# Storing the low parts of the first MLP's and the first pointwise convolution's weights in DRAM at their first use, and loading them at the second

## The chip, the cores and the metric

One core of a Trainium2 chip runs the whole program. The metric is the device time in microseconds (us). The profile is of one execution of that core; its engines are PE (TensorE, matrix products), DVE (VectorE), ACT (ScalarE), POOL (GpSimd) and SP (SyncE, which here only issues DMA transfers).

## The reference, cut to what matters

A network of two layers over 1024 tokens with 1024 channels, in float32. Layer 0 is a hybrid mixer (RWKV-7 time mixing beside sliding-window attention) and an MLP; layer 1 is a Conformer convolution and an MLP; a last rmsnorm ends it. The change touches the weights of these two parts:

```python
def conformer_conv(h, pw1_w, pw1_b, dw_w, dw_b, ln_g, ln_b, pw2_w, pw2_b):
    u = h @ pw1_w + pw1_b                                     # 1024 -> 2048
    u = u[..., :D_MODEL] * jax.nn.sigmoid(u[..., D_MODEL:])
    u = <depthwise convolution of 31 taps over tokens>(u, dw_w) + dw_b
    u = jax.nn.silu(<layer norm>(u))
    return u @ pw2_w + pw2_b

def sqrelu_mlp(h, w1, w2):                                    # 1024 -> 4096 -> 1024
    return jnp.square(jax.nn.relu(h @ w1)) @ w2
```

## The kernel before

Activations lie feature-major: a tile holds 128 channels by 512 tokens, so the 1024 tokens are worked on as two halves. To keep float32 accuracy each operand of a product is split into a high part in the reduced format (`hi`, a cast on ACT, L286 for weights) and a low part (`lo = x - hi`, the subtraction at L271 on DVE or POOL), and each product is three: high by high, high by low, low by high (`mm3`, L299 to L301).

Weights are never kept. `weights` (L273) loads a block in two **pieces** of 128x512 (256 KB each, from SP's queue), casts each on ACT into `whi` and subtracts into `wlo` on DVE or POOL. `wraw`, `whi` and `wlo` are rings of four slots, one piece each. A piece feeds twelve products. Which engine subtracts is set by `dve`: True is DVE, False is POOL, None lets a counter `nlo` choose DVE two times in three.

Since each half of the tokens goes through the network on its own, each weight is loaded and split twice. The order of the program from about 500 us on is

- the MLP of layer 0 on the first half (`mlp(0, x0)`, subtractions by the counter), woven on PE with the recurrence scans and the attention of both halves, to about 1040 us;
- `conv_in` of the first half (the first pointwise product, 16 blocks, and the gate `u`, L1217);
- the MLP of layer 0 on the second half (`mlp(0, x1)`, subtractions all on POOL), from 1151.65 to about 1563 us. Beside it DVE runs `conv`, the 31 taps (L1223 and L1226) of eight channel blocks, 240 of them L1226, for the first half, and then the layer norm, whose first product on PE is L1239;
- `conv_out` of the first half, and `conv_in` of the second half from about 1607 us;
- the MLP of layer 1 on the first half (its other weights, on POOL as well) from about 1699 us, with the second half's taps beside it on DVE; then the rest, to 2519 us.

An MLP goes by blocks of 512 hidden channels. `first` makes four hidden tiles of 24 products each (called F below): ACT squares them, and the low part `hidl` is subtracted at L271 on POOL. `second` makes eight output tiles in pairs of 24 products (called S0S1 to S6S7); each is added by DVE into `x` at L1183, an addition with one operand in PSUM and one in SBUF, after which its PSUM slot is free. There are six slots. The order in PE's queue is F0 F1 of the next block, S0 to S7 of this one, F2 F3 of the next one; so S6 may start when DVE has added S0, F2 when it has added S2, and the next F0 when it has added S4.

The order of each queue is settled when the kernel is built (on PE by hand to 1040 us, else by the scheduler), and no engine changes it while it runs. On POOL stands also L1457, which copies the last 30 columns of a finished `u` to its front, as soon as the taps of that channel block are done.

Of the kernel before, what the change touches and what calls it, by code (L numbers as in the profile page):

```python
# [9 lines left out]
F32 = mybir.dt.float32  # L10
F32R = mybir.dt.float32r
# [6 lines left out]
P = 128  # L18
# [15 lines left out]
class Ring:  # L34
    """slots taken in turn, from one or several pools"""
# [10 lines left out]
class Net:  # L46
    def __init__(self, ctx, tc, A, out):
        self.ctx, self.tc, self.nc, self.A, self.out = ctx, tc, tc.nc, A, out
        self.nlo = 0
        self.clk = 0.0  # L50
        self.done = set()
        self.natt = 0
        self.open = []

# [17 lines left out]
    # ---------------------------------------------------------------- order on the tensor engine  # L72
    def go(self, gen):
        """a stream on its own"""
        while True:
            try:
                next(gen)
            except StopIteration as e:
                return e.value

    def weave(self, base, *gens):
        """several streams in one order: the first of gens that is due goes on, base between them, so that the array
        stays busy; a stream yields the time (us) that its next products have to wait for the other engines, or the
        name of what has to be there"""
# [22 lines left out]
    # ---------------------------------------------------------------- constants  # L107
# [62 lines left out]
    def warm(self):  # L170
        """products that nobody reads, while the array would only wait: so its clock stays up for the first columns"""
# [92 lines left out]
    # ---------------------------------------------------------------- helpers  # L264
    def lo(self, out, x, hi, dve=None):
        """out = x - hi, for the second part of an operand"""
# [6 lines left out]
    def weights(self, aps, a, b, dve=None):  # L273
        """blocks of weights in two parts, k by k; loaded and split one half of them after the other"""
        nc = self.nc
        h = a // 2
        if dve is None:
# [3 lines left out]
        for i in range(2):  # L281
            for ap, (his, los) in zip(aps, ws):
                raw = self.wraw.tile([P, h, b], F32, "wraw")
                nc.sync.dma_start(out=raw, in_=ap[:, i * h:(i + 1) * h, :])
                hi = self.whi.tile([P, h, b], F32R, "whi")
                nc.scalar.copy(out=hi, in_=raw)  # L286
                lo = self.wlo.tile([P, h, b], F32R, "wlo")
                self.lo(lo, raw, hi, dve)
# [4 lines left out]
    def weight(self, ap, a, b, dve=None):  # L293
        return self.weights([ap], a, b, dve)[0]
# [27 lines left out]
    def norm_first(self, hf, rows, dst):  # L322
        """first rmsnorm by rows, then turned to feature-major; dst(u, g): where the two parts go"""
# [42 lines left out]
    def first_stored(self):  # L366
        """the second half's first norm, kept in DRAM until its place is free"""
# [20 lines left out]
    def colsum(self, xs, sq, k="n"):  # L388
        """sum over channels of x (or of its square), in two parts"""
# [29 lines left out]
    def rstd(self, accs, eps, pool, k="n"):  # L419
        """1 / sqrt(mean + eps) for every token, on every partition"""  # L420
# [56 lines left out]
    # ---------------------------------------------------------------- input projection  # L477
# [10 lines left out]
    def w_in_pair(self, js, hs):  # L488
        """two columns side by side, channel block by channel block: what is there first is used first"""
# [31 lines left out]
    # ---------------------------------------------------------------- rwkv  # L521
    def scan(self, hf, p, r, k, v, la, gl, sset, ptag, ahead):
# [86 lines left out]
        # unit lower triangular inverse: 16-blocks by substitution, then two merges  # L609
# [97 lines left out]
        # per chunk: state' = M state + C, output = R state + Y  # L707
# [114 lines left out]
    # ---------------------------------------------------------------- attention  # L822
    def attention(self, hf, i, z, qs, mi):
        """query heads 2i and 2i+1"""
# [54 lines left out]
    # ---------------------------------------------------------------- mixer of one half  # L879
# [14 lines left out]
    def shift(self, hf, j, ps, keep=False, hp=False):  # L894
        """one 128-channel column of the input projection of the rwkv part, shifted"""
# [18 lines left out]
    def twice(self, j, rows, cols, width):  # L914
        """64 channels of a column, on both halves of the partitions; cols: (from, of which half's column) pieces"""
# [6 lines left out]
    def att_in(self, hf):  # L922
        """keys with one block of the half before in front: the high part of each kv head on both halves of the
        partitions, the low parts of the first on the upper one and of the second on the lower one; values by rows"""
# [23 lines left out]
    def queries(self, hf, i, z):  # L948
        """two heads' queries, each with its high part on the half of the partitions where the low part of its keys is
        and its low part on the other one"""  # L950
# [10 lines left out]
    def att(self, hf, z):  # L961
        """attention of one half: query heads 4z to 4z+3"""
# [26 lines left out]
    def cols0(self, hs):  # L989
        """the first half's input projection"""  # L990
# [23 lines left out]
    def last1(self, h1):  # L1014
        """the last two columns, under the norm"""
# [20 lines left out]
    def scans(self, z, todo):  # L1036
        """scans one after the other in one set of tiles"""
# [39 lines left out]
    def w_out(self, hf, mi, xs, w_):  # L1077
        """output projection; the second half's input is there, the first half's comes along;
        the first half's first two columns begin with what is done, while the last scan and the attention go on"""
# [56 lines left out]
    # ---------------------------------------------------------------- mlp  # L1136
    def mlp(self, layer, halves, blocks, ahead, dve=None, close=None):
        """halves: list of (x tiles, (hi, lo)); blocks of 512 hidden channels;
# [365 lines left out]
```

## Time and profile before

| | us |
|---|---|
| three timed runs | 2516.49, 2522.08, 2525.11 (median 2522.08) |
| profiled execution, span of the instructions | 2519.2 |
| PE busy | 2355.4 (93%) |
| DVE busy | 1568.6 (62%) |
| ACT busy | 1055.3 (42%) |
| POOL busy | 843.9 (33%) |
| DMA, mean rate | 94 GB/s, 236.19 MB |

The page gives no time of the profiled execution beside its span, which lies among the three runs, 2.9 us under their median. On the page the span is cut into 40 slices of 63 us; a digit is the busy share in tenths, PEclk the granted clock of TensorE. A busy PE is one whose products overlap; the count of products in a stretch tells more than its busy share, and a chain or a wait names the instruction that was waited for.

### The profile page before, as it was taken

The numbers are of one execution on the slowest core, as the hardware profiler recorded it, in microseconds if no ns is written. First come the engines' busy times: TensorE is split into PE (matmuls) and PEld (weight loads), VectorE is DVE, ScalarE is ACT, GpSimd is POOL, SyncE is SP. The second block draws the span as 40 slices with busy tenths as digits, with TensorE's granted clock in tenths as the row PEclk, the third lists the DMA queues.
The fourth block names the chain that finished last, engine by engine and source line by source line (L and its number), as shares of the span: only waits on it lengthen the run. The fifth ranks groups of instructions, "written<-read, shape, count | busy, mean of one in ns | idle before, by whom it ended". The sixth has DMA issues, their size and how long they took to land.

```text
span 2519.2 us, 38162 instructions
## 1 busy us (share of the span) xinstructions
PE 2355.4 (93%) x14525; PEld 1875.1 (74%) x14525; DVE 1568.6 (62%) x2613; ACT 1055.3 (42%) x1888; POOL 843.9 (33%) x676
## 2 busy tenths in 40 slices
PE   7999899899999999999678999997779999999998
PEld 6776677767777778777566888876657888888887
DVE  6766745647573646499998403899998025533333
ACT  6546645445352424344223543523225434433333
POOL 2223333111111112126547664226456643212221
PEclk9999999989999999999898999999889999999999
DMA  6435324313122223323112333332222332433332
GB/s 210 115 108 147 93 67 147 101 58 90 56 70 85 74 81 101 101 84 101 59 59 76 101 98 99 93 88 84 67 67 80 101 100 88 127 100 96 97 99 85
DMA packets 371851, 236.19 MB, mean 94 GB/s; under 512 B 39522, under 2 KB 355156, under 8 KB 371668
## 3 DMA queue, kind: packets, MB, share of 16 engines
q1 hardware_dynamic: 367604, 225.89, 30.2%
q0 software_dynamic: 2176, 4.19, 0.6%
q10 hardware_dynamic: 1888, 3.67, 0.4%
q8 instruction: 114, 1.87, 0.3%
q14 instruction: 69, 0.57, 0.1%
HBM read 215.35 MB, written 18.35 MB: 93 GB/s over the span
## 4 chain that ended last, share of the span: by engine, by line
PE 64%; DVE 28%; ACT 3%; DMA 3%; issue 2%; SPq 0%; POOL 0%; ACTq 0%; DVEq 0%; POOLq 0%
PE mm L299 19%; PE mm L300 18%; PE mm L301 18%; DVE acc L1226 17%; DVE x L1183 1%; DVE wlo L271 1%; DVE nt L472 1%; PE sc L603 1%; DMA raw<-p 1%; PE sc L685 1%; DVE E L662 1%; DVE C L660 1%; DVE h L271 1%; PE sc L768 1%; PE at L842 1%
## 5 line engine op out<-in xcount | busy, mean ns | idle before, releaser
L271 POOL TENSOR_TENSOR wlo<-wraw,whi 128x512 fp32r<-128x512 f32 x448 | 630.6, 1411 | 1293.6 <-ACT whi L286 1223.3
L286 ACT CAST whi<-wraw 128x512 fp32r<-128x512 f32 x720 | 445.1, 620 | 1065.8 <-PE mm L300 911.0
L299 PE MATMUL mm<-h,whi 128*128 128x512 f32 x1792 | 730.3, 408 | 10.7 <-DVE x L1183 7.1
L301 PE MATMUL mm<-h,wlo 128*128 128x512 f32 x1792 | 707.2, 395 | 7.5 <-DVE wlo L271 7.5
L300 PE MATMUL mm<-h,whi 128*128 128x512 f32 x1792 | 706.4, 394 | 0.5 <-DVE h L271 0.3
L299 PE MATMUL mm<-hidh,whi 128*128 128x512 f32 x992 | 396.0, 401 | 77.0 <-DVE x L1183 75.4
L1226 DVE SCALAR_TENSOR_TENSOR acc<-u,par,acc 128x512 f32<-128x512 f32 x480 | 466.7, 1030 | 0.1
L299 PEld LDWEIGHTS mm<-h,whi 128*128 128x128 f32 x1792 | 340.5, 190 | 93.6 <-issue 18.1
L301 PEld LDWEIGHTS mm<-h,wlo 128*128 128x128 f32 x1792 | 340.4, 190 | 85.3 <-DVE wlo L271 11.6
L301 PE MATMUL mm<-hidh,wlo 128*128 128x512 f32 x992 | 389.8, 395 | 11.2 <-POOL wlo L271 11.2
L300 PEld LDWEIGHTS mm<-h,whi 128*128 128x128 f32 x1792 | 341.3, 190 | 67.8 <-issue 2.0
L300 PE MATMUL mm<-hidl,whi 128*128 128x512 f32 x992 | 390.0, 394 | 0.3 <-DVE hidl L271 0.2
L1183 DVE TENSOR_TENSOR x<-mm,x 128x512 f32<-128x512 f32 x248 | 167.6, 685 | 291.9 <-PE mm L301 291.7
L271 DVE TENSOR_TENSOR wlo<-wraw,whi 128x512 fp32r<-128x512 f32 x272 | 194.6, 717 | 202.7 <-ACT whi L286 194.4
L299 PEld LDWEIGHTS mm<-hidh,whi 128*128 128x128 f32 x992 | 189.3, 191 | 123.1 <-issue 80.7
L301 PEld LDWEIGHTS mm<-hidh,wlo 128*128 128x128 f32 x992 | 189.1, 191 | 52.2 <-POOL wlo L271 11.6
L300 PEld LDWEIGHTS mm<-hidl,whi 128*128 128x128 f32 x992 | 189.6, 191 | 39.8 <-issue 1.1
L271 POOL TENSOR_TENSOR hidl<-rel,hidh 128x512 fp32r<-128x512 f32 x77 | 113.1, 1468 | 44.3 <-ACT hidh L1162 25.1
L1158 ACT ACTIVATE rel<-rel 128x512 f32<-128x512 f32 x128 | 80.6, 632 | 3.5
L1157 ACT ACTIVATE rel<-mm 128x512 f32<-128x512 f32 x128 | 75.5, 592 | 5.9 <-DVE u L1217 4.8
L1164 DVE CAST hidh<-rel 128x512 fp32r<-128x512 f32 x68 | 31.4, 464 | 52.5 <-ACT rel L1158 52.4
L473 ACT CAST h<-nt 128x512 fp32r<-128x512 f32 x48 | 29.7, 621 | 56.9 <-DVE nt L472 56.5
(357 smaller groups left out, 2257.3 us busy)
## 6 DMA issues: line engine op xcount, KB each, us to landing
wraw<-in_mlp_w_dram SPq DMA_DIRECT2D x512, 256.0 KB
wraw<-in_cv_pw_w_dram SPq DMA_DIRECT2D x96, 256.0 KB
wraw<-in_hy_w_in_dram SPq DMA_DIRECT2D x80, 256.0 KB
wraw<-in_hy_w_out_dram SPq DMA_DIRECT2D x32, 256.0 KB
p<-stg SPq DMA_DIRECT2D x30, 256.0 KB
raw<-p SPq DMA_DIRECT2D x40, 128.0 KB
krv<-p SPq DMA_DIRECT2D x18, 256.0 KB
xrow<-in_x_dram SPq DMA_DIRECT2D x8, 512.0 KB
```

Of the source, the lines that this page charges most:

```text
L271: eng.tensor_tensor(out=out, in0=x, in1=hi.bitcast(F32), op=ALU.subtract)
L286: nc.scalar.copy(out=hi, in_=raw)
L299: mm(ps, lhsT=whi, rhs=xhi, start=start, stop=False)
L300: mm(ps, lhsT=whi, rhs=xlo, start=False, stop=False)
L301: mm(ps, lhsT=wlo, rhs=xhi, start=False, stop=stop)
L472: nc.vector.scalar_tensor_tensor(out=t, in0=xs[c], scalar=self.pv(gname, c), in1=r, op0=ALU.mult, op1=ALU.mult)
L473: nc.scalar.copy(out=his[c], in_=t)
L1157: nc.scalar.activation(out=t, in_=ps, func=AF.Relu)
L1158: nc.scalar.activation(out=t, in_=t, func=AF.Square)
L1164: nc.vector.tensor_copy(out=hi, in_=t)
L1183: nc.vector.tensor_tensor(out=x, in0=pss[o], in1=x, op=ALU.add)
L1226: nc.vector.scalar_tensor_tensor(out=acc, in0=u[:, j:j + H], scalar=self.pv(f"dw{j}", c), in1=acc, op0=ALU.mult, op1=ALU.add)
```

## The change

`weights` gets a mode `keep`. With "put" it does what it did, and then SP also writes each low piece into a DRAM tile of its own (256 KB). With "get" it loads the piece and casts the high part as before, and takes the low part by a second DMA from that DRAM tile instead of the subtraction. `mlp(0, x0)` and the first half's `conv_in` put, `mlp(0, x1)` and the second half's `conv_in` get: 128 and 32 pieces. In "get" the counter `nlo` isn't advanced. Nothing else is computed in another way.

```diff
     def weights(self, aps, a, b, dve=None, keys=None, keep=None):
         nc = self.nc
         h = a // 2
-        if dve is None:
+        if dve is None and keep != "get":
             self.nlo += 1
             dve = self.nlo % 3 != 0
         ws = [([], []) for _ in aps]
         for i in range(2):
-            for ap, (his, los) in zip(aps, ws):
+            for n, (ap, (his, los)) in enumerate(zip(aps, ws)):
                 raw = self.wraw.tile([P, h, b], F32, "wraw")
                 nc.sync.dma_start(out=raw, in_=ap[:, i * h:(i + 1) * h, :])
+                lo = self.wlo.tile([P, h, b], F32R, "wlo")
+                if keep == "get":
+                    nc.sync.dma_start(out=lo.bitcast(F32), in_=self.los.pop((keys[n], i)))
                 hi = self.whi.tile([P, h, b], F32R, "whi")
                 nc.scalar.copy(out=hi, in_=raw)
-                lo = self.wlo.tile([P, h, b], F32R, "wlo")
-                self.lo(lo, raw, hi, dve)
+                if keep != "get":
+                    self.lo(lo, raw, hi, dve)
+                if keep == "put":
+                    d = self.dp.tile([P, h, b], F32, name="lo", tag=f"lo{len(self.los)}", bufs=1)
+                    self.los[keys[n], i] = d
+                    nc.sync.dma_start(out=d, in_=lo.bitcast(F32))
...
-            yield from self.mlp(0, [(self.x0, n0)], range(8), 0)
+            yield from self.mlp(0, [(self.x0, n0)], range(8), 0, keep="put")
...
-        self.go(self.mlp(0, [(x1, self.norm(x1, "nf0", 1))], range(8), 2, False))
+        self.go(self.mlp(0, [(x1, self.norm(x1, "nf0", 1))], range(8), 2, False, keep="get"))
...
+            keep = "get" if hf else "put"
-            whi, wlo = self.weight(w[:, :, (NK + c) * P:(NK + c + 1) * P], NK, P)
+            whi, wlo = self.weight(w[:, :, (NK + c) * P:(NK + c + 1) * P], NK, P, None, (3, NK + c), keep)
```

The new lines shift the line numbers: L271, L286, L1183, L1217, L1226 and L1457 of before are L272, L291, L1192, L1227, L1236 and L1467 after; a get is issued at L289, a put at L297.

POOL's queue beside the first half's taps (`wlo` is the low part of a weight, `hidl` that of a hidden tile, `u` the gated input of the taps). Before:

```order
L271 TENSOR_TENSOR hidl_12170<-rel_12166,hidh_12169 128x512
L271 TENSOR_TENSOR wlo_12261<-wraw_12257,whi_12259 128x512
L271 TENSOR_TENSOR wlo_12267<-wraw_12263,whi_12265 128x512
L271 TENSOR_TENSOR hidl_12214<-rel_12210,hidh_12213 128x512
L271 TENSOR_TENSOR wlo_12301<-wraw_12297,whi_12299 128x512
L271 TENSOR_TENSOR wlo_12307<-wraw_12303,whi_12305 128x512
L1457 COPY u_11199<-u_11199 128x30
L271 TENSOR_TENSOR wlo_12341<-wraw_12337,whi_12339 128x512
```

After:

```order
L272 TENSOR_TENSOR hidl_12490<-rel_12486,hidh_12489 128x512
L272 TENSOR_TENSOR hidl_12534<-rel_12530,hidh_12533 128x512
L1467 COPY u_11455<-u_11455 128x30
L272 TENSOR_TENSOR hidl_12738<-rel_12734,hidh_12737 128x512
L272 TENSOR_TENSOR hidl_12782<-rel_12778,hidh_12781 128x512
L272 TENSOR_TENSOR hidl_12826<-rel_12822,hidh_12825 128x512
L272 TENSOR_TENSOR hidl_12870<-rel_12866,hidh_12869 128x512
L1467 COPY u_11456<-u_11456 128x30
```

The weights' subtractions are gone, and the hidden tiles' ones and the copies stand next to each other. DVE's and PE's queues are the same, row for row, over the whole of this stretch.

SP's queue in the MLP of layer 0 on the second half (`wraw` is the loaded piece, `lo` the DRAM tile). Before:

```order
L284 DMA wraw_12041<-in_mlp_w1_dram 128x4x128
L284 DMA wraw_12047<-in_mlp_w1_dram 128x4x128
L284 DMA wraw_12085<-in_mlp_w1_dram 128x4x128
L284 DMA wraw_12091<-in_mlp_w1_dram 128x4x128
L284 DMA wraw_12129<-in_mlp_w1_dram 128x4x128
```

After:

```order
L289 DMA wlo_12319<-lo_5941 128x512
L286 DMA wraw_12405<-in_mlp_w1_dram 128x4x128
L289 DMA wlo_12325<-lo_5949 128x512
L286 DMA wraw_12411<-in_mlp_w1_dram 128x4x128
L289 DMA wlo_12363<-lo_6020 128x512
L286 DMA wraw_12449<-in_mlp_w1_dram 128x4x128
```

Each piece now has a get between two loads; a load stands right behind the get of the piece four before it. In the parts that put, writes and loads alternate in the same way.

DVE's queue at the end of the second half's `conv_in`, up to the first addition of the MLP that follows (`acc` is the sum of the taps). Before:

```order
L1217 SCALAR_TENSOR_TENSOR u<-mm,par,sig 128x512
L1226 SCALAR_TENSOR_TENSOR acc<-u,par,acc 128x512 x6
L1223 TENSOR_SCALAR acc<-u,par 128x512
L1226 SCALAR_TENSOR_TENSOR acc<-u,par,acc 128x512 x8
L1217 SCALAR_TENSOR_TENSOR u<-mm,par,sig 128x512
L1226 SCALAR_TENSOR_TENSOR acc<-u,par,acc 128x512 x7
L1223 TENSOR_SCALAR acc<-u,par 128x512
L1226 SCALAR_TENSOR_TENSOR acc<-u,par,acc 128x512 x45
L1183 TENSOR_TENSOR x_4833<-mm,x_4833 128x512
```

After:

```order
L1227 SCALAR_TENSOR_TENSOR u<-mm,par,sig 128x512
L1236 SCALAR_TENSOR_TENSOR acc<-u,par,acc 128x512 x6
L1233 TENSOR_SCALAR acc<-u,par 128x512
L1236 SCALAR_TENSOR_TENSOR acc<-u,par,acc 128x512 x9
L1227 SCALAR_TENSOR_TENSOR u<-mm,par,sig 128x512
L1236 SCALAR_TENSOR_TENSOR acc<-u,par,acc 128x512 x7
L1233 TENSOR_SCALAR acc<-u,par 128x512
L1236 SCALAR_TENSOR_TENSOR acc<-u,par,acc 128x512 x45
L1192 TENSOR_TENSOR x_4833<-mm,x_4833 128x512
```

These rows are alike but for one more tap; ahead of them 21 subtractions of weights are gone from DVE's queue, so that 97 taps instead of 82 stand before the block of 45. Behind it the taps between the additions number 98 instead of 113, and on PE the layer norm's first product (L1239, after it L1249) stands 62 products earlier in this stretch than it did.

## Rows read from the trace of the kernel before

**Rows 1.** Stretches: length, busy time (count) of each engine, granted clock, DMA share, GB/s

```profile
0.00:50.00 50.00, 36.59 (x165) 30.40 (x166) 32.74 (x75) 33.12 (x58) 14.53 (x37) 0.93 0.62 192
510.00:1042.00 532.00, 526.39 (x4044) 404.42 (x4042) 300.74 (x679) 230.84 (x437) 88.18 (x81) 0.98 0.27 80
1152.00:1363.00 211.00, 162.73 (x673) 131.93 (x672) 210.15 (x223) 61.86 (x103) 128.39 (x79) 0.89 0.23 71
1363.00:1570.00 207.00, 207.00 (x902) 170.28 (x901) 67.73 (x81) 96.12 (x160) 121.54 (x92) 0.99 0.31 96
1699.00:1903.00 204.00, 151.60 (x636) 123.45 (x636) 203.97 (x214) 57.04 (x95) 106.73 (x68) 0.87 0.24 72
```

**Rows 2.** Waits of PE from 1152 to 1363 us: total, times, longest

```profile
PE mm L299 <- DVE x L1183: 33.2, 4, 18.3
PE mm L301 <- POOL wlo L271: 11.2, 1, 11.2
PE lnl L1239 <- DVE acc L1238: 3.9, 1, 3.9
```

**Rows 3.** PE's timeline: start, length; in brackets the idle time before it

```profile
1151.65 0.39 PE L299 MATMUL mm<-h,whi 128*128 128x512 f32 x1
1151.88 0.39 PE L300 MATMUL mm<-h,whi 128*128 128x512 f32 x1
...
1362.31 2.08 PE L1239 MATMUL lnl<-acc,ones 128*128 128x512 f32 x2 [3.88 <-DVE acc L1238]
```

**Rows 4.** DVE's timeline in the same stretch

```profile
1169.19 0.74 DVE L1217 SCALAR_TENSOR_TENSOR u<-mm,par,sig 128x512 f32<-128x512 f32 x1
...
1180.46 37.83 DVE L1226 SCALAR_TENSOR_TENSOR acc<-u,par,acc 128x512 f32<-128x512 f32 x46
1218.22 0.67 DVE L1183 TENSOR_TENSOR x<-mm,x 128x512 f32<-128x512 f32 x1
...
1301.50 15.31 DVE L1226 SCALAR_TENSOR_TENSOR acc<-u,par,acc 128x512 f32<-128x512 f32 x12
...
1317.33 10.02 DVE L1226 SCALAR_TENSOR_TENSOR acc<-u,par,acc 128x512 f32<-128x512 f32 x15
```

**Rows 5.** POOL's timeline: first and last of five rows, seven subtractions

```profile
1302.93 1.79 POOL L271 TENSOR_TENSOR hidl<-rel,hidh 128x512 fp32r<-128x512 f32 x1
...
1313.19 1.75 POOL L271 TENSOR_TENSOR hidl<-rel,hidh 128x512 fp32r<-128x512 f32 x1
```

**Rows 6.** POOL's groups from 1152 to 1363 us: busy, mean ns, idle before

```profile
L271 POOL TENSOR_TENSOR wlo<-wraw,whi 128x512 fp32r<-128x512 f32 x56 | 90.9, 1635 | 22.5 <-ACT whi L286 22.3
L271 POOL TENSOR_TENSOR hidl<-rel,hidh 128x512 fp32r<-128x512 f32 x15 | 24.9, 1658 | 4.0 <-ACT hidh L1162 4.0
```

**Rows 7.** DVE's groups from 1152 to 1363 us

```profile
L1226 DVE SCALAR_TENSOR_TENSOR acc<-u,par,acc 128x512 f32<-128x512 f32 x189 | 188.8, 1061 | 0.0
L1183 DVE TENSOR_TENSOR x<-mm,x 128x512 f32<-128x512 f32 x24 | 16.1, 676 | 0.0
```

**Rows 8.** Waits of PE from 1699 to 1903 us

```profile
PE mm L299 <- DVE x L1183: 49.3, 3, 23.4
PE lnl L1239 <- DVE acc L1238: 3.1, 1, 3.1
```

**Rows 9.** DVE's timeline there, the block of 45 taps

```profile
1718.40 0.73 DVE L1217 SCALAR_TENSOR_TENSOR u<-mm,par,sig 128x512 f32<-128x512 f32 x1
...
1728.25 42.31 DVE L1226 SCALAR_TENSOR_TENSOR acc<-u,par,acc 128x512 f32<-128x512 f32 x45
```

**Rows 10.** The chain in order of time: start, length; transfers of 256 KB, the last of 128 KB

```profile
3.17 7.20 DMA wraw<-in_hy_w_in_dram
...
51.51 2.88 DMA wraw<-in_hy_w_in_dram
56.40 4.61 DMA hd<-xl
...
502.10 2.97 DMA raw<-p
```

More of the change, by code (lines that the diff above doesn't have):

```diff
@@ L53, in __init__ @@
         self.open = []
+        self.los = {}
     def pool(self, name, bufs=1, space=None, side=None):
@@ L271, in lo, with weights @@
         eng.tensor_tensor(out=out, in0=x, in1=hi.bitcast(F32), op=ALU.subtract)
-    def weights(self, aps, a, b, dve=None):
+    def weights(self, aps, a, b, dve=None, keys=None, keep=None):
         nc = self.nc
         h = a // 2
-        if dve is None:
+        if dve is None and keep != "get":
             self.nlo += 1
@@ L291, in weights, with weight @@
         return ws
-    def weight(self, ap, a, b, dve=None):
-        return self.weights([ap], a, b, dve)[0]
+    def weight(self, ap, a, b, dve=None, key=None, keep=None):
+        return self.weights([ap], a, b, dve, [key], keep)[0]
     def mm3(self, ps, whi, wlo, xhi, xlo, start, stop):
@@ L1134, in w_out, with mlp @@
         return xs
-    def mlp(self, layer, halves, blocks, ahead, dve=None, close=None):
+    def mlp(self, layer, halves, blocks, ahead, dve=None, close=None, keep=None):
         nc = self.nc
@@ L1149, in first @@
                 f = fb * 4 + ft
-                whi, wlo = self.weight(w1[:, :, f * P:(f + 1) * P], NK, P, dve)
+                whi, wlo = self.weight(w1[:, :, f * P:(f + 1) * P], NK, P, dve, (1, f), keep)
                 for hh, (xs, (his, los)) in zip(hid, halves):
@@ L1171, in second @@
             for oc in range(4):
-                whi, wlo = self.weight(w2[:, fb * 4:fb * 4 + 4, oc * 256:(oc + 1) * 256], 4, 256, dve)
+                whi, wlo = self.weight(w2[:, fb * 4:fb * 4 + 4, oc * 256:(oc + 1) * 256], 4, 256, dve, (2, fb, oc), keep)
                 for hh, (xs, _) in zip(hid, halves):
@@ L1209, in conv_in @@
             nc.scalar.activation(out=t, in_=ps, func=AF.Sigmoid, bias=self.pv("b1", NK + c))
-            whi, wlo = self.weight(w[:, :, c * P:(c + 1) * P], NK, P)
+            whi, wlo = self.weight(w[:, :, c * P:(c + 1) * P], NK, P, None, (3, c), keep)
             ps = self.mmps()
```

## The prediction

> **What bounds the kernel now.** I read the stretches first [rows 1]. Over most of the span PE has no gap: from 1363 to 1570 us it is busy for all of 207 us at a clock of 0.99, and there a faster DVE or POOL buys nothing. Two stretches differ: 1152 to 1363 and 1699 to 1903 us, beside the taps of the two halves. There DVE is busy throughout (210.15 of 211 us), PE runs 673 products, and the clock falls to 0.89 and 0.87. A product starts 0.227 us after the one before [rows 3], so 672 products, the number from the MLP's first at 1151.65 to the norm's at 1362.31, need 152.3 us. They took 210.7: 58.4 us are lost, 48.3 of them as waits [rows 2], the rest as products at the lower clock just after a wait. The waits second: PE waits for the addition into x, for one subtraction on POOL and for the end of the taps [rows 2]. The longest shows the pattern: PE stops for 18.3 us [rows 2], since the addition that frees its PSUM slot stands in DVE's queue behind a block of 46 taps, and the block takes 37.83 us [rows 4].
>
> Third, why the block takes so long. Fifteen taps in a row take 10.02 us, 0.668 each; twelve take 15.31 [rows 4], and beside these twelve POOL makes seven subtractions [rows 5], beside the fifteen none. The excess is 15.31 - 12 x 0.668 = 7.3 us, **1.04 us for each subtraction on POOL**. Over the whole stretch 189 taps take 188.8 us [rows 7] in place of 126.3; the excess of 62.5 over 71 subtractions [rows 6] is 0.88 each. The additions into x, with only one operand in SBUF, keep to 0.67 beside all this [rows 4, 7]. So POOL's work, idle as POOL looks, is paid by DVE, and DVE's lateness is paid by PE.
>
> The Trainium skill, "SBUF — State Buffer", section "Who interferes with whom", says that a VectorE instruction with two SBUF inputs contends with a GpSimd instruction that reads SBUF, and that the loser is blocked for the whole of the other's instruction. The rows agree on which instructions are hit, but not on the size: 1.04 us against a subtraction of 1.6 us [rows 5, 6]. By the whole instruction 56 subtractions would give back 90 us, more than PE has lost; the time would then be the one at PE's bound, worked out below as the range's lower side.
>
> **The first half's taps: the term that counts.** The get takes POOL's subtractions of weights out of this stretch: 56 of its 71 [rows 6], and four more between 1144 and 1152 us. DVE's and PE's orders there stay as they are, so each tap and addition can be shifted by what is gone ahead of it. Eighteen of the 60 lie ahead of the first addition at 1218.22 [rows 4]: at 1.04 that brings it to 1199.5. PE wants it after six F and three pairs, 9 x 24 x 0.227 = 49 us after 1151.65, at 1200.7. The wait of 18.3 us is all but gone, with the low clock behind it. The block can't start at once, though: the last gate (1169.19 now [rows 4]) needs PE's product of 1151.65, and with the ten subtractions ahead of it gone it comes at 1158.8, so nothing there runs dry. In the next block S0 is added behind 35 taps (23.4 us, four hidden subtractions, 4.2): DVE reaches it about 1248, PE wants it about 1247. In the third, 31 taps and the hidden ones give about 1292 against 1292. So PE and DVE run nearly level, with one or two us lost at each block.
>
> The end: DVE's last tap comes 60 x 0.88 = 53 us earlier, at 1309 (60 x 1.04 = 62: 1300). PE alone would arrive at 1151.65 + 152.3 = 1304. With the short waits I put the norm's first product at 1312: **50 us gained**. At most it is 58 (PE's own pace). At least 40: the 15 hidden subtractions stay, and if each cost its whole 1.66 us [rows 6] in place of 1.04, 9 us would go. The copies at L1457 now stand between hidden subtractions, each waiting for taps; the nearest hidden tile behind one is needed by PE more than 10 us later, as F2 and F3 and the next F0 and F1 come between, so I cost them at nothing; if that cover were gone, see the first rival. From 1363 to 1570 the cleared POOL is worth nothing, PE being full.
>
> **The gets.** A slot of `wlo` falls free when PE has used the piece four back; then SP issues the get, and PE needs it three pieces later, 36 x 0.227 = 8.2 us. SP issues the load behind it at the same beat as before, since the cast waits for the same piece. Transfers of 256 KB land in 2.9 to 4.6 us, one in 7.2 at the crowded start [rows 10]. The engines are busy at 0.31 with 96 GB/s [rows 1]; twice that is 0.62, which the first 50 us show as a rate that runs (0.62 at 192 GB/s). Cost nothing; the margin is 1 to 5 us a piece.
>
> **The puts.** A put waits for its subtraction, and the load right behind it on SP waited for that same subtraction already, to have its raw slot back. So nothing new is queued behind a wait; what is added is a second issue and 256 KB of traffic ahead of the small transfers of scans and attention. From 510 to 1042 us PE is busy for 526.39 of 532 us, and only 0.27 of the DMA share is used [rows 1]; but near 502 us the chain runs through such a transfer [rows 10]. Bounds: 0, and 8 us if some eight transfers on that chain came a whole us later; I take 3, nearer to nothing, for PE's queue has other work there.
>
> **The second half's conv_in and taps.** Here the subtractions of the MLP's weights stay. In conv_in 21 subtractions leave DVE (at 0.67, 14 us) and 11 leave POOL (11 us), and 97 taps, not 82, are done ahead of the block. Now the last gate comes at 1718.40 [rows 9], 19 us after PE has its product at 1699; I let it come 8 us after, 11 earlier. But in that time POOL makes three subtractions to every F (5.44 us), which leave DVE 43% of its pace: 5 us of progress, off the wait of 23.4 us [rows 8]. The two later waits lose 1 to 3 us of taps; yet PE's norm product stands 62 products (14 us) earlier and waits for the last tap itself, which costs 2 more than the 3.1 us it waits now. Together with conv_in's own short waits on DVE I take **5 us gained**, from 15 (all 11 us and the rest) down to a loss of 8 (nothing earlier, and PE held longer at the norm).
>
> **Sum.** 50 + 5 - 3 = 52 us. From the span, 2519.2 - 52 = 2467; the span lies 2.9 us under the median of the runs, so from 2522 the time is **2470 us**.
>
> **Rivals.**
> *The wait moves to the hidden tiles.* If taps stay slower than 0.668, or the copies hold up the hidden subtractions behind them, PE waits for `hidl` instead. For it: 3.9 us at the end of the taps and 11.2 us for a POOL subtraction are waited for even now [rows 2]. Against: the 10 us of cover above. Four places with copies, some 6 us each, cut the 50 to 25: 2495 us.
> *It does nothing.* If the slow taps came not from these subtractions but from traffic or from the hidden ones alone, the gain would be only conv_in's, lost again by the puts: 2520 us. Against: seven excesses of the same size beside seven subtractions, four of them of weights.
> *Slower: the gets come late.* Place: SP's queue from 1152 to 1563 us and in conv_in. If a get landed later than 8.6 us (8.2 and the two products ahead of the first that needs it), each four pieces would be late by the rest, 40 times over 160 pieces. At 10.3 us that is 68 us, more than the 52 gained: 2538 us. It decides from 9.9 us on. Against: only one transfer of the chain comes near [rows 10].
> The Trainium skill speaks for this one: "SBUF — State Buffer", section "A bandwidth-pool intuition that's wrong (but worth ruling out)", calls HBM almost always the bottleneck end to end, and the change adds some 84 MB to the 236 moved. Here it would act by the late landing just priced; the rows show a third of the DMA engines' time in use, which speaks against it.
>
> **How the numbers follow.** Forecast 0.75, hidden tiles 0.12, nothing 0.07, late gets 0.06. The range goes from all of PE's loss and the best of conv_in without a cost (58 + 15: 2449) to the least of each (40 - 8 - 8 = 24: 2498), which takes in the first rival. About 0.3%, 7.6 us, is what a measurement here can tell from no change: faster by more 0.87, within 0.07, slower 0.06.
>
> **What would show it.** After: taps of 0.67 us but for one in ten or so, 15 subtractions on POOL beside them; the block of 46 in 34 to 37 us; PE's waits from 1152 us to the norm under 10 us in place of 48 and a clock over 0.95 there; the norm's first product about 1312 us plus what the first half has cost; the second half's taps still with three long waits. I am wrong if taps stay at 1.06, if PE waits for DMA into `wlo`, or if the first half ends more than 8 us later.

## The result, and the profile after

| | before | after |
|---|---|---|
| median of the timed runs, us (four of each) | 2519.28 | 2453.19 |
| ratio, 95% interval | | 0.9739 [0.9716, 0.9761] |
| profiled execution, span | 2519.2 | 2453.9 |
| PE busy | 2355.4 | 2343.1 |
| DVE busy | 1568.6 | 1483.5 |
| POOL busy | 843.9 | 640.9 |
| DMA, mean rate, GB/s; MB | 94; 236.19 | 130; 320.12 |

The changed kernel is 2.6% faster, 2453 us where 2470 was forecast and 2449 to 2498 given as the range, near its lower end. By the spans, 65.3 us are gone where 52 were summed up.

Stretches of the changed kernel, with the columns of [rows 1]: the first half's taps, the 208 us behind them, the second half's taps.

```profile
1152.00:1312.00 160.00, 154.70 (x676) 126.30 (x674) 158.50 (x220) 62.27 (x103) 43.04 (x23) 0.99 0.66 194
1311.00:1519.00 208.00, 208.00 (x903) 170.90 (x903) 59.70 (x81) 96.09 (x160) 29.70 (x22) 0.99 0.59 179
1643.00:1834.00 191.00, 145.88 (x611) 118.64 (x610) 189.07 (x201) 57.89 (x96) 101.11 (x66) 0.87 0.24 72
```

The first answers the third row of [rows 1]: as many products on PE (676 against 673) in 160 us in place of 211, at a clock of 0.99 in place of 0.89; POOL is busy for 43 us in place of 128; DVE is full in both. The third is still what it was: a clock of 0.87, POOL busy for 101 us.

PE's waits (total, times, longest), first from 1152 to 1312 us, against [rows 2]:

```profile
PE lnl L1249 <- DVE acc L1248: 3.2, 1, 3.2
PE mm L308 <- DVE x L1192: 2.0, 2, 1.2
```

then from 1643 to 1834 us, against [rows 8]:

```profile
PE mm L308 <- DVE x L1192: 31.6, 2, 19.3
PE lnl L1249 <- DVE acc L1248: 13.5, 1, 13.5
```

In the first stretch 48.3 us of waits have become 5.2. In the second, four waits have become three, 52.4 us have become 45.1. Groups of DVE and POOL from 1152 to 1312 us (busy, mean ns), against [rows 6, 7]:

```profile
L1236 DVE SCALAR_TENSOR_TENSOR acc<-u,par,acc 128x512 f32<-128x512 f32 x186 | 138.7, 809 | 0.0
L272 POOL TENSOR_TENSOR hidl<-rel,hidh 128x512 fp32r<-128x512 f32 x15 | 28.2, 1887 | 58.0 <-ACT hidh L1171 54.3 <-issue 3.7
```

The 56 subtractions of weights are gone from POOL, the 15 of hidden tiles stay, and a tap takes 0.81 us on the mean in place of 1.06. Rows of DVE's timeline there (start, length), against [rows 4]:

```profile
1158.94 0.73 DVE L1227 SCALAR_TENSOR_TENSOR u<-mm,par,sig 128x512 f32<-128x512 f32 x1
...
1165.67 35.78 DVE L1236 SCALAR_TENSOR_TENSOR acc<-u,par,acc 128x512 f32<-128x512 f32 x46
1201.37 0.68 DVE L1192 TENSOR_TENSOR x<-mm,x 128x512 f32<-128x512 f32 x1
```

and of PE's, against the last of [rows 3]:

```profile
1310.66 1.22 PE L1249 MATMUL lnl<-acc,ones 128*128 128x512 f32 x1 [3.19 <-DVE acc L1248]
```

The last gate comes at 1158.94 (forecast 1158.8), the block of 46 takes 35.78 us (34 to 37), the first addition comes at 1201.37 (1199.5), and the norm's first product at 1310.66 (1312; before 1362.31).

What each place gave is read by pairing the n-th product of PE in the two traces. The first product of the second half's MLP stands at 1151.8 us, 0.2 later than before; the norm's first one 51.7 earlier; behind it the lead stays at 51.3 us up to 1607 us of before. It grows to 55.4 in the second half's `conv_in`, to 60.2 at the first long wait, 61.0 at the second, 64.2 behind the norm and 65.1 at the end. So the first half's taps gave 51.7 us, and all behind 1607 us gave 13.8: 4.1 in `conv_in`, 4.8 and 0.8 at the two long waits, 3.2 at the norm, 0.9 behind it.

### The profile page after: what moved, and what is told of

Its sections match the earlier page's. It is cut to its first block, busy times and chain, and to the rows that moved or that the text cites. A ratio compares the mean times of both kernels' runs of the same rounds, so it can differ in the third digit from the quotient of the medians.

```text
span 2453.9 us, 38633 instructions
## 1 busy us (share of the span) xinstructions
PE 2343.1 (95%) x14525; PEld 1867.9 (76%) x14525; DVE 1483.5 (60%) x2595; ACT 1056.3 (43%) x1888; POOL 640.9 (26%) x534
## 2 busy tenths in 40 slices
DMA packets 417934, 320.12 MB, mean 130 GB/s; under 512 B 44642, under 2 KB 360276, under 8 KB 417748
## 4 chain that ended last, share of the span: by engine, by line
PE 69%; DVE 24%; ACT 3%; DMA 2%; issue 1%; SPq 0%; POOL 0%; DVEq 0%; ACTq 0%; POOLq 0%
PE mm L308 21%; PE mm L309 19%; PE mm L310 19%; DVE acc L1236 15%; DVE x L1192 1%; PE sc L612 1%; DMA raw<-p 1%; PE sc L694 1%; PE at L851 1%; PE sc L777 1%; PE at L883 1%; DVE nt L481 1%; DVE C L669 1%; PE sc L731 1%; DVE wlo L272 1%
## 5 line engine op out<-in xcount | busy, mean ns | idle before, releaser
L291 ACT CAST whi<-wraw 128x512 fp32r<-128x512 f32 x720 | 445.6, 620 | 1012.2 <-PE mm L309 907.0
L272 POOL TENSOR_TENSOR wlo<-wraw,whi 128x512 fp32r<-128x512 f32 x302 | 413.3, 1370 | 1188.2 <-ACT whi L291 1103.8
L1236 DVE SCALAR_TENSOR_TENSOR acc<-u,par,acc 128x512 f32<-128x512 f32 x480 | 404.4, 902 | 0.2
L1192 DVE TENSOR_TENSOR x<-mm,x 128x512 f32<-128x512 f32 x248 | 167.8, 686 | 288.3 <-PE mm L310 288.0
L272 DVE TENSOR_TENSOR wlo<-wraw,whi 128x512 fp32r<-128x512 f32 x258 | 184.9, 718 | 199.3 <-ACT whi L291 187.2
L272 POOL TENSOR_TENSOR hidl<-rel,hidh 128x512 fp32r<-128x512 f32 x79 | 118.2, 1498 | 244.7 <-ACT hidh L1171 178.0
L272 POOL TENSOR_TENSOR h<-nt,h 128x512 fp32r<-128x512 f32 x15 | 27.5, 1834 | 95.9 <-ACT h L482 93.3
```

The lines of the kernel that those rows point to most:

```text
L272: eng.tensor_tensor(out=out, in0=x, in1=hi.bitcast(F32), op=ALU.subtract)
L1192: nc.vector.tensor_tensor(out=x, in0=pss[o], in1=x, op=ALU.add)
L1236: nc.vector.scalar_tensor_tensor(out=acc, in0=u[:, j:j + H], scalar=self.pv(f"dw{j}", c), in1=acc, op0=ALU.mult, op1=ALU.add)
```

## The experiments

The theory: a subtraction on POOL holds up a tap on DVE by about 1.04 us, the additions that PE wants stand behind the taps, and the loads help since they take that work off POOL. The rivals: the gain comes from PE not waiting for POOL's low parts and from shorter queues; any work of POOL slows the taps; the two parts of the change don't do what the sum gives to each; and the puts cost something that the gains cover. For each kernel a ratio stands against runs of the kernel before beside it, with its 95% interval.

### The parts of the change

**Only the MLP puts and gets.**

```diff
-            keep = "get" if hf else "put"
+            keep = None
```

> Only the MLP of layer 0 puts and gets; conv_in subtracts in both halves, as in the kernel before. The theory: the gain beside the first half's taps is all the MLP's, so the norm's first product comes some 52 us earlier and stays 51 us earlier up to the second half's taps; there the waits are those of before (23.4, 12.9 and 13.1 us). Time about 2467 us, 52 less than before. The rival: the 13 us that the changed kernel gains behind 1700 us also come from the first half's lead (other scheduling behind the MLP), not from conv_in's gets: about 2455 us, with a first long wait of 19 us as in the changed kernel.

2470.04 us, 0.9806 [0.9785, 0.9827]. The norm's first product stands at 1312.12 us, the lead is 49.7 us from there to 1699 us of before and 49.2 at the end. PE's waits beside the second half's taps:

```profile
PE mm L308 <- DVE x L1192: 49.4, 3, 23.4
PE lnl L1249 <- DVE acc L1248: 3.0, 1, 3.0
```

These are the rows of [rows 8] again to 0.1 us: the MLP's loads give nothing there.

**Only `conv_in` puts and gets.**

```diff
-            yield from self.mlp(0, [(self.x0, n0)], range(8), 0, keep="put")
+            yield from self.mlp(0, [(self.x0, n0)], range(8), 0)
...
-        self.go(self.mlp(0, [(x1, self.norm(x1, "nf0", 1))], range(8), 2, False, keep="get"))
+        self.go(self.mlp(0, [(x1, self.norm(x1, "nf0", 1))], range(8), 2, False))
```

> Only conv_in of the two halves puts and gets; the MLP subtracts as in the kernel before. The theory that conv_in's gets made all that the changed kernel gained behind 1607 us: nothing changes to 1600 us, then some 4 us are gained in conv_in and some 9 to 10 beside the second half's taps: about 2506 us. The rival, the term on record of 5 us, with the rest due to the MLP: about 2514 us. If the gets of conv_in do nothing by themselves: 2519 us.

2506.47 us, 0.9951 [0.9934, 0.9969]: 13.4 us by the medians. In the first half the waits of before are still there (47 us); PE's waits from 1695 to 1881 us are those of the changed kernel:

```profile
PE mm L308 <- DVE x L1192: 31.7, 2, 19.3
PE lnl L1249 <- DVE acc L1248: 13.5, 1, 13.5
```

So the two parts add up within the intervals (49.8 + 13.4 = 63.2 by the medians, 66 for both together), and the 13 us belong to `conv_in`. The recorded term of 5 us was too small, not the MLP's too large.

**The puts alone.**

```diff
-            keep = "get" if hf else "put"
+            keep = None if hf else "put"
...
-        self.go(self.mlp(0, [(x1, self.norm(x1, "nf0", 1))], range(8), 2, False, keep="get"))
+        self.go(self.mlp(0, [(x1, self.norm(x1, "nf0", 1))], range(8), 2, False))
```

> The puts alone: all 160 pieces are written to DRAM at their first use, and nothing loads them; the second half subtracts as in the kernel before, so the outputs are the same and only traffic and DMA issues are added. The theory: the puts are hidden (the product at the head of the second half's MLP came only 0.2 us later in the changed kernel): within 1 us of before, about 2519 us. The rival: they cost 3 to 8 us somewhere that the gains behind them cover: 2522 to 2527 us.

2517.47 us, 1.0001 [0.9986, 1.0016]: no cost that can be seen; a cost of 3 us would still lie inside the interval, one of 5 would not. Moving 160 pieces of 256 KB out to DRAM took the rate from 510 to 1042 us from 80 to 141 GB/s, and PE lost nothing beside it: by the pairing of products its place against the kernel before is 7.0 us late ahead of the first put and 5.6 at the head of the second half's MLP.

**Loads for the first four of the MLP's eight blocks only.**

```diff
-                whi, wlo = self.weight(w1[:, :, f * P:(f + 1) * P], NK, P, dve, (1, f), keep)
+                whi, wlo = self.weight(w1[:, :, f * P:(f + 1) * P], NK, P, dve, (1, f), keep if fb < 4 else None)
```

(and the same for the second product's weights)

> As the changed kernel, but the MLP puts and gets only the weights of the first four of its eight blocks of 512 hidden channels, those used beside the first half's taps; the other four blocks subtract as in the kernel before. The theory: behind the taps PE is full anyway, so the other blocks' gets are worth nothing: 2453 us, within 3 of the changed kernel, the norm's first product at 1311 us. The rival: clearing POOL is worth something there too (PE ran at less than its pace behind the norm): 5 us or more of the gain are lost, 2458 us or more.

2455.10 us, 0.9742 [0.9721, 0.9764]; the changed kernel had 0.9739. The 208 us behind the norm, where POOL subtracts 64 weights again:

```profile
1314.00:1522.00 208.00, 208.00 (x906) 170.65 (x907) 65.47 (x81) 96.78 (x162) 111.73 (x84) 0.99 0.35 106
```

906 products in 208 us, with POOL busy for 112 us; 903 with POOL busy for 30. Half of the MLP's round trips are worth nothing that these runs can measure: where PE is full for all of the stretch, POOL's work costs PE nothing.

### Is it POOL's work, and what of it

**The same subtraction as a dummy.** Beside each get of the MLP, POOL subtracts into a tile that nothing reads.

```diff
+                if keep == "get" and keys[n][0] < 3:
+                    j = self.jp.tile([P, h, b], F32, name="junk", tag="junk")
+                    nc.gpsimd.tensor_tensor(out=j, in0=raw, in1=hi.bitcast(F32), op=ALU.subtract)
```

> The changed kernel, and beside each of the 128 gets of the second half's MLP POOL also makes the subtraction that the get replaced, into a tile that nothing reads: the outputs are the same, no product waits for it, and only POOL's work beside the taps is back. The theory that POOL's two-operand work slows DVE's taps by about 1.04 us each: the taps from 1152 us on take about 1.0 us again, PE waits some 45 us for DVE, and the norm's first product comes at 1350 to 1362 us: 2497 to 2505 us. The rival, that the gain came from PE no longer waiting for POOL's low parts and from shorter queues: taps at 0.7 us, 2453 to 2458 us.

2503.97 us, 0.9941 [0.9918, 0.9964]: the MLP's gain is gone, and about `conv_in`'s is left (0.9951 alone). DVE's group from 1157 to 1368 us (busy, mean ns):

```profile
L1239 DVE SCALAR_TENSOR_TENSOR acc<-u,par,acc 128x512 f32<-128x512 f32 x188 | 189.2, 1070 | 0.0
```

POOL's group there:

```profile
L296 POOL TENSOR_TENSOR junk<-wraw,whi 128x512 f32<-128x512 f32 x57 | 90.0, 1580 | 28.0 <-ACT whi L291 15.6 <-issue 4.9 <-POOL junk L296 3.5
```

PE's waits there:

```profile
PE mm L311 <- DVE x L1195: 31.4, 4, 19.3
PE mm L313 <- DMA wlo<-lo: 14.7, 4, 11.5
```

The taps are back at 1.07 us and 31.4 us of waits for additions are back (33.2 before), though no product needs these results: for these waits the rival that the gain was PE's own waiting for POOL has fallen. DVE's queue is the changed kernel's, row for row. The last row was not expected, and it is no work of the taps. The dummy holds the raw slot as the real subtraction did, so the next load of a raw piece waits on SP (55 times for the dummy, 141 us together), the get behind it comes late, and PE waits for `wlo` by a DMA where the kernel before waited for POOL [rows 2]. That is the late get of the prediction's third rival; it appears as soon as something keeps a raw slot.

**POOL writes but doesn't read.** In place of the subtraction, POOL fills the raw piece with zeros once the cast has read it.

```diff
+                if keep == "get" and keys[n][0] < 3:
+                    nc.gpsimd.memset(raw, 0.0)
```

> The changed kernel, and beside each of the 128 gets of the second half's MLP POOL writes zeros over the loaded piece once the cast has read it (128x512, no operand read): the outputs are the same. The theory that a tap is slowed by POOL's reads of SBUF: taps stay near 0.7 us and the time at 2453 to 2460 us. The rival, that any work of POOL on a tile slows the taps for as long as it runs: the taps' excess is about 0.6 of the fill's duration for each fill, some 25 us or more over the stretch: 2475 us or more.

2451.43 us, 0.9729 [0.9713, 0.9745], as the changed kernel. DVE's group from 1152 to 1312 us:

```profile
L1238 DVE SCALAR_TENSOR_TENSOR acc<-u,par,acc 128x512 f32<-128x512 f32 x180 | 134.6, 812 | 0.0
```

POOL's:

```profile
L295 POOL MEMSET wraw<- 128x512 f32 x54 | 27.9, 526 | 59.0 <-ACT whi L291 37.0 <-issue 19.8 <-POOL wraw L295 1.2
```

54 fills, 28 us of POOL's time, and the taps stay at 0.81 us (0.809 without them). So it isn't that POOL is busy or writes; what is left is what the subtraction does and a fill doesn't, reading its operands from SBUF and computing. The Trainium skill, "SBUF — State Buffer", section "Who interferes with whom", names the reading: a VectorE instruction with two SBUF inputs contends with a GpSimd one that reads SBUF, not with one that only writes. Both runs agree with it, but none here has POOL read without computing. The fill holds the raw slot too, and PE waits 5.2 us for two late gets here, where the changed kernel has no such wait.

**A dummy of half the size.** The dummy subtraction takes 128x256.

```diff
+                    j = self.jp.tile([P, h, b], F32, name="junk", tag="junk")
+                    q = (slice(None), slice(0, h // 2), slice(None))
+                    nc.gpsimd.tensor_tensor(out=j[q], in0=raw[q], in1=hi.bitcast(F32)[q], op=ALU.subtract)
```

> As the kernel with a dummy subtraction on POOL beside each load (2504 us, taps of 1.07 us), but the dummy takes only half of the piece, 128x256. If a subtraction on POOL costs DVE a fixed time, one tap that takes 1.04 us longer, whatever its length: taps of 1.0 to 1.07 us and 2495 to 2505 us. If the cost goes by its length: taps of about 0.94 us, PE's waits half as long, 2475 to 2485 us.

2476.26 us, one run. DVE's group from 1149 to 1333 us:

```profile
L1240 DVE SCALAR_TENSOR_TENSOR acc<-u,par,acc 128x512 f32<-128x512 f32 x188 | 159.0, 910 | 0.0
```

POOL's:

```profile
L297 POOL TENSOR_TENSOR junk<-wraw,whi 128x256 f32<-128x256 f32 x56 | 56.9, 1017 | 44.9 <-ACT whi L291 21.7 <-issue 15.2 <-PE mm L314 5.4
```

One tap in DVE's timeline:

```profile
1269.78 1.23 DVE L1240 SCALAR_TENSOR_TENSOR acc<-u,par,acc 128x512 f32<-128x512 f32 x1
```

and the dummy beside it in POOL's:

```profile
1269.65 0.80 POOL L297 TENSOR_TENSOR junk<-wraw,whi 128x256 f32<-128x256 f32 x1 [1.61 <-ACT whi L291]
```

A tap alone takes 0.73 us in this view (one starts 0.66 after the other); this one takes 0.50 more. By the groups: 188 taps at a pace of 0.668 are 125.6 us, so the excess is 33.4; the 15 hidden subtractions take 15.6 of it at 1.04, and 17.8 are left for 56 dummies, 0.32 each on the mean. In full size the excess was 189.2 - 125.6 = 63.6 for 72 subtractions, 0.88 each. So the cost goes by the size of POOL's instruction. The taps' mean of 0.91 us and the time are those of that theory; a fixed cost per instruction has fallen. Of PE's waits in this stretch, 14.8 us are for additions and 11.4 for late gets, so the time is not the taps' alone.

What a subtraction takes with no tap beside it is seen behind the norm. First full size (the run with whole dummies, from 1375 to 1570 us), then half (this run, from 1340 to 1525 us); least, median and most in ns:

```profile
L296 POOL TENSOR_TENSOR junk<-wraw,whi x67: 1282/1292/1750, 1375.5 to 1558.6; 128x512 f32<-128x512 f32 x67
L297 POOL TENSOR_TENSOR junk<-wraw,whi x67: 729/738/1191, 1340.8 to 1521.3; 128x256 f32<-128x256 f32 x67
```

Against 1.29 and 0.74 us alone, a tap is held up by 1.04 and 0.50: in both sizes some 0.25 us less than the subtraction takes by itself. What POOL's rows show above 1.29 us beside the taps is POOL's own delay there, so their length is no measure of what DVE pays.

### Clearing POOL without DRAM

**Layer 1's weights on DVE too.** With the loads kept, the weights of layer 1's MLP beside the second half's taps are subtracted on DVE.

```diff
-        self.go(self.mlp(1, [(x0, n0)], range(7), 2, False))
+        self.go(self.mlp(1, [(x0, n0)], range(7), 2, False, wdve=True))
```

(`wdve or dve` takes the place of `dve` where `mlp` loads its weights)

> The changed kernel, but the weights of layer 1's MLP on the first half, which stand beside the second half's taps, are subtracted on DVE in place of POOL: the same 128x512 subtractions on the other engine. By the excess of 1.04 us for each on POOL against 0.67 us for one on DVE, some 54 of them save 54 x 0.37 = 20 us of DVE's time in the stretch, and with POOL clear the waits shrink: 2435 to 2445 us. The rival: a subtraction on DVE stands behind a block of taps in its queue, and PE then waits for low parts rather than for additions: 2470 us or more.

2406.24 us, 0.9550 [0.9536, 0.9565]. 47 us below the changed kernel, twice what DVE's account gave. The stretch from 1638 to 1800 us, columns as in [rows 1]:

```profile
1638.00:1800.00 162.00, 158.41 (x682) 126.56 (x681) 162.00 (x230) 61.72 (x104) 27.39 (x15) 1.00 0.30 91
```

DVE's groups in it:

```profile
L1236 DVE SCALAR_TENSOR_TENSOR acc<-u,par,acc 128x512 f32<-128x512 f32 x144 | 116.3, 849 | 0.0
L272 DVE TENSOR_TENSOR wlo<-wraw,whi 128x512 fp32r<-128x512 f32 x57 | 38.7, 679 | 0.0
```

PE's longest sum of waits in it:

```profile
PE mm L310 <- DVE wlo L272: 3.0, 6, 1.0
```

682 products in 162 us at full clock, where the changed kernel made 611 in 191. DVE is as full as before, but 57 subtractions cost it 38.7 us in place of 57 x 1.04 = 59; that is 21 us. Beside that its order has changed: between the additions of one block and of the next stand 25 taps in place of 32, and PE's norm stands 192 products later, so the taps are no longer all wanted at once. The taps aren't done sooner: the last one ends at 1817.9 us, 2.9 before the changed kernel's. But PE has made 192 products more by then, at 0.227 us each 44 of the 47 us. No run separates what DVE saves from what the order gives.

**The same with the dummies on POOL.** The orders of PE, DVE and ACT are those of the kernel just shown; only POOL's subtractions beside the second half's taps are back, unread.

```diff
+                if keys and keys[n] and keys[n][0] < 3 and dve and keep is None and self.dum:
+                    j = self.jp.tile([P, h, b], F32, name="junk", tag="junk")
+                    nc.gpsimd.tensor_tensor(out=j, in0=raw, in1=hi.bitcast(F32), op=ALU.subtract)
```

> The kernel with the loads and layer 1's weights on DVE (2406 us), and POOL also makes each of layer 1's subtractions there, into a tile that nothing reads; the orders of PE, DVE and ACT are those of the 2406 us kernel, row for row. Theory A: that kernel is fast because POOL no longer slows the taps: with some 55 dummies at 1.04 us each DVE loses 57 us beside the second half's taps, PE waits again, 2440 us or more. Theory B: it is fast because the additions into x stand earlier in DVE's order: 2406 to 2420 us.

2474.23 us, 0.9821 [0.9791, 0.9850], 68 us above. DVE's groups from 1644 to 1860 us:

```profile
L1239 DVE SCALAR_TENSOR_TENSOR acc<-u,par,acc 128x512 f32<-128x512 f32 x145 | 156.3, 1119 | 0.0
L272 DVE TENSOR_TENSOR wlo<-wraw,whi 128x512 fp32r<-128x512 f32 x57 | 50.8, 892 | 0.0
```

POOL's:

```profile
L296 POOL TENSOR_TENSOR junk<-wraw,whi 128x512 f32<-128x512 f32 x57 | 89.3, 1567 | 100.2 <-ACT whi L291 96.0 <-POOL junk L296 2.4 <-PE mm L313 1.7
```

PE's longest sum of waits:

```profile
PE mm L313 <- DVE wlo L272: 38.4, 31, 3.3
```

Theory A holds: with the order unchanged, 57 dummies at 1.04 are 59 of the 68 us. DVE's own subtractions, which have two operands in SBUF as the taps do, are slowed with them (0.89 against 0.68 us). The better order alone is not enough: with POOL's reads back the kernel is 21 us slower than the changed one.

**No DRAM: the first stretch's weights on DVE.** The kernel before, with the second half's MLP of layer 0 subtracting on DVE.

```diff
-        self.go(self.mlp(0, [(x1, self.norm(x1, "nf0", 1))], range(8), 2, False, keep="get"))
+        self.go(self.mlp(0, [(x1, self.norm(x1, "nf0", 1))], range(8), 2, False, wdve=True))
```

(no `keep` anywhere)

> No DRAM round trip at all: the kernel before, with the weights of the second half's MLP of layer 0 (beside the first half's taps) subtracted on DVE in place of POOL. It asks what the loads bring beyond clearing POOL. If only DVE's time counts: 56 subtractions cost 0.61 us each of DVE's pace there and save 1.04, 24 us of the 52: about 2495 us. If, as the kernel with layer 1's weights on DVE showed (48 us gained where DVE's account gave 20), subtractions on DVE also change where the scheduler puts taps and additions, so that PE's additions no longer stand behind blocks of taps: about 2470 us, as with the loads.

2468.35 us, 0.9808 [0.9770, 0.9845]: as with the MLP's loads alone (0.9806). The stretch from 1141 to 1310 us:

```profile
1141.00:1310.00 169.00, 160.33 (x678) 125.17 (x677) 169.00 (x241) 61.14 (x103) 29.75 (x19) 1.00 0.30 89
```

DVE's taps in it:

```profile
L1236 DVE SCALAR_TENSOR_TENSOR acc<-u,par,acc 128x512 f32<-128x512 f32 x155 | 123.5, 840 | 0.0
```

PE's longest sum of waits in it:

```profile
PE mm L310 <- DVE wlo L272: 7.7, 12, 1.6
```

Nothing is stored, and PE gets its products in 169 us (160 with the loads, 211 before). 155 taps stand in it in place of 186, and 31 behind it in DVE's queue. Here too the order has changed: the norm's first product stands 205 products later on PE, and the last tap ends at 1351 us (1359 before). This traced execution was 10.6 us ahead of the kernel before at the MLP's first product already, so the taps are not done sooner; PE only wants them later. By the pairing the stretch gave 45 us, and 52 with the MLP's loads.

**No DRAM, both stretches.** As the one before, and

```diff
-        self.go(self.mlp(1, [(x0, n0)], range(7), 2, False))
+        self.go(self.mlp(1, [(x0, n0)], range(7), 2, False, wdve=True))
```

> As the one before, and also layer 1's MLP on the first half (beside the second half's taps) on DVE; conv_in as in the kernel before; nothing is put into DRAM. If subtractions on DVE do what the loads do: about 2415 to 2425 us (2406 with the loads, without what conv_in's loads gave). If the loads are needed because DVE is full beside the taps: 2450 us or more.

2424.43 us, 0.9622 [0.9588, 0.9655], 29 us below the changed kernel without any of its 320 transfers.

**And with `conv_in`'s loads.** The same, with 32 pieces stored and loaded in place of 160.

```diff
-            keep = None
+            keep = "get" if hf else "put"
```

> The kernel with both stretches' weights on DVE (2424 us), and conv_in of the two halves puts and gets as in the changed kernel: 32 pieces in DRAM in place of 160. It asks what the MLP's 128 round trips are worth once DVE could make the subtractions: 2406 us with them. If conv_in's loads are what DVE lacked (they gave 13 us alone): 2408 to 2412 us, so the MLP's loads are worth some 4 us. If DVE is the limit beside the first half's taps, where it still makes 57 subtractions at 0.61 us: 2418 us or more.

2419.02 us, 0.9608 [0.9585, 0.9630]. 13 us above the kernel with the MLP's loads as well: the second of the two cases. By the pairing of products 8 of these arise beside the first half's taps, where DVE's subtractions make PE wait. `conv_in`'s loads gave 5 us here by the medians, whose intervals overlap, and 11 behind 1607 us by the pairing.

## Why the prediction was right, point by point

**What bounds the kernel** (DVE's taps beside POOL's subtractions, PE behind DVE): right. The dummies put taps, waits and time back, the fills didn't, and the loads that lie where PE is full were worth nothing, as said of 1363 to 1570 us.

**1.04 us for each subtraction, by the rows and not the whole instruction:** right in size. In the changed kernel ten taps of DVE's timeline

```profile
1221.84 8.79 DVE L1236 SCALAR_TENSOR_TENSOR acc<-u,par,acc 128x512 f32<-128x512 f32 x10
```

and two hidden subtractions beside them in POOL's show it:

```profile
1222.24 1.50 POOL L272 TENSOR_TENSOR hidl<-rel,hidh 128x512 fp32r<-128x512 f32 x1 [3.46 <-ACT hidh L1171]
1227.68 1.74 POOL L272 TENSOR_TENSOR hidl<-rel,hidh 128x512 fp32r<-128x512 f32 x1 [3.94 <-ACT hidh L1171]
```

Ten taps alone are 9 x 0.663 + 0.73 = 6.70 us; 8.79 leaves 2.09, 1.04 for each, beside instructions of 1.50 and 1.74 us. In the trace one tap takes the whole of each excess, 1.04 and 1.03. By the Trainium skill, "SBUF — State Buffer", section "SBUF: two separate sides", the one of the two that comes second is blocked for the whole of the other's instruction. By that the two would have cost, estimated, 3.2 us by these lengths, and 2.6 by the 1.29 us that each takes with no tap beside it; the rows show 2.09. The prediction set 1.04 against 1.6 us, a length that holds POOL's own delay. Against 1.29 its 56 subtractions come to 72 us in place of 90, still more than PE had lost.

**The first half's taps, 50 us:** 51.7. Its steps held within 2 us each (gate, block, addition, norm, in the rows above). The waits left are 5.2 us, within the ten allowed.

**The copies and hidden tiles cost nothing:** right, PE waits for no `hidl` there.

**The gets cost nothing:** right for the changed kernel; it waits for no `wlo` from 1152 to 1643 us, at a DMA share of 0.66 (0.62 was foreseen). The dummies show how little lies behind that: 14.7 us of waits once the raw slots are held longer.

**The puts, 3 us:** nothing that can be measured. The pair of traces differs by 1.1 us ahead of the first put and by 0.2 behind the MLP's last; the puts alone cost at most some 4 by their interval. Too dear by up to 3, inside its bounds (0 to 8).

**The second half's `conv_in` and taps, 5 us: the mis-sized term.** It gave 13.8 in the traces, 13.4 alone. Two steps failed. First, `conv_in`'s own waits on DVE, which I had named without a price. From 1600 to 1699 us PE waited in the kernel before:

```profile
PE mm L301 <- DVE wlo L271: 2.5, 5, 0.6
```

In the changed kernel it waits for nothing in that stretch, and 4.1 us are gone there. Second, the end: I took 1 to 3 us off the two later waits and let the norm's wait come on top, 2 us longer, since its product stands 62 products earlier. In place of 13.05 and 3.1 us, the third block's wait and the norm's, there is now one (PE's timeline):

```profile
1822.34 1.22 PE L1249 MATMUL lnl<-acc,ones 128*128 128x512 f32 x1 [13.47 <-DVE acc L1248]
```

The last sum of the taps and the third block's addition now stand next to each other in DVE's queue (1821.59 and 1822.20 us), so PE, which waits for the first, waits no more for the second and pays once: 3.2 us gained there. The first wait shrank as said (23.4 to 19.3, forecast 5 off); the second shrank by 0.6 where 1 to 3 were forecast.

**The rivals:** moved waits, nothing and late gets all failed in the changed kernel.

## What to carry to other kernels

A subtraction moved to an idle engine isn't free when the full engine's instructions have two operands in SBUF: divide the excess of the full engine's instructions by the count on the other engine, and weigh it against making the work on the full engine itself (here 1.04 us against 0.61 to 0.68). Storing and reloading a result was one way to clear POOL (52 us in the first stretch); subtracting on DVE, with another order of its queue and PE's, gave 45 there with no transfer; and loads in the first stretch with DVE in the second, 2406 us, was the best of what was run. When two waits end at neighbouring instructions of one queue, count them once.

## What the runs showed of the hardware

- A 128x512 subtraction on POOL held up one tap on DVE by 1.04 us whether POOL's own row gave 1.50 or 1.74 us; one of 128x256 by 0.50. With no tap beside them they take 1.29 and 0.74 us, some 0.25 more than the tap loses in either size.
- A fill on POOL (0.53 us for 128x512, no operand) did not slow the taps: 0.812 against 0.809 us.
- Going from 71 to 194 GB/s beside the taps, with the DMA share from 0.23 to 0.66, did not slow the taps (0.663 us apart against 0.668) or PE (676 products in 160 us at a clock of 0.99).
